# Three edits around waits in a two-layer decoder trunk: a norm matmul four blocks later, a normalization spread over more blocks, a rearranged end

## The chip, the cores and the metric

One core of one Trainium2 chip. The metric is the device time of one execution in microseconds, given as the median of several runs. The core has a matmul engine (PE, with its weight loads PEld), a vector engine (DVE), an activation engine (ACT), GpSimd (POOL) and a queue engine (SP) that issues transfers. Each engine works through its own instructions in order and waits on semaphores for the others.

## What is computed

Two layers over 256 tokens of width 2048, all in fp32. Layer 0 mixes with attention heads and gated linear attention, layer 1 with a Mamba-2 mixer; after each comes a squared-ReLU MLP and a per-layer input embedding, and at the end a norm:

```python
for i in range(DEPTH):
    hn = rms_norm(h, norm_mix[i])
    h = h + (sb_gla_mixer if i % 2 == 0 else ssd_mixer)(hn, ...)
    h = h + squared_relu_mlp(rms_norm(h, norm_mlp[i]), mlp_w_up[i], mlp_w_down[i])
    h = h + sigmoid(h @ ple_w_gate[i]) * (p[i] @ ple_w_proj[i])
return rms_norm(h, final_norm)
# in ssd_mixer, before the output projection:
#   z, xbc, dt = split(hn @ w_in); xbc = silu(causal_conv(xbc)); y = scan(xbc, softplus(dt))
#   y = rms_norm((y + d * xs) * silu(z), norm_g);  return y @ w_out
```

A norm is a row's values times `rstd`, one number per token (the reciprocal root of the mean square), times a gain per column. Since `rstd` is one number per token, a projection may be taken first of the values with the gain alone and be multiplied by `rstd` afterwards. The kernel uses that in places: `xu` holds the layer's input with the gain but without `rstd`, `x` holds it with both.

## The kernel before

Every fp32 product is made of three reduced-precision products: a weight block is split into a high part (`whi`, a cast on ACT, line 84) and the remainder (`wlo`, a subtraction on DVE, line 85), and the activations were split in the same way earlier (`split_into`, a scaled copy on ACT, line 105, and a multiply-subtract on DVE, line 106). So each 128x1024 piece of weights that PE uses needs one pass of ACT and then one of DVE. Three buffers each hold `whi` and `wlo`.

The weights stream through two loops. `feature_major` (PE lines 124 and 129) gives transposed results, four PSUM banks for each group of 512 columns, out of a pool of five banks; `token_major` (PE lines 153 to 155) gives rows, two banks for each group. Both are generators that yield after every block of 1 MB of weights and once more after a group's evacuation. `pace` drives such a generator and, after each of its yields, advances a list of side generators by one step: `[start, every, generator]`. That is how normalization, convolution, scan and statistics are laid between the weight blocks. The order of the text is a wish only: a scheduler that works at compile time orders the instructions of each engine by readiness in its own model, so that an instruction which depends on nothing can move far ahead.

Second mixer (`mixer1`). Its steps are counted in yields of `main`. Yields 1 to 5 are the first group (B), 6 to 10 the second (C), 11 and 12 the `dt` block, all three on `xu`, with the results multiplied by `rstd` afterwards (lines 166 and 167). Yields 13 to 17 are the first group of `xs`, on `x`, and all later groups use `x`. `norm_x` starts at yield 2: it makes `rstd` out of the sums of squares (`h_rstd`, `rstd_rows`), and then `normalize` makes `x`: for each of 16 slices one multiplication on POOL (`hn`, line 258) and one `split_into`. Two slices are made for each yield, in yields 4 to 11. Beside it run the convolution steps of B and C (`conv_silu`, lines 505 to 510), the `dt` chain (`dt_steps`, lines 466 to 494, on DVE) and, from yield 18, the scan of group 0 (`group`).

Pages of 8 KB per partition come from one pool of 12 (`pages`): four for `x`, four for `xu`, two for `raw`, one each for `bc`, `dt_work`, `rb`, `mt` and so on.

End of the second mixer. `sq_acc`, the sum of squares of the gated result, is built up by `gated` on POOL (line 181). `y_rstd` (line 673) sums it over channels by a matmul with one column (line 676) and makes `r_y`. It is carried over into the output projection as a side that starts at its first yield. `r_y` is read by the first evacuation there, after eight blocks (line 311).

The end. In the second layer's `ple`, each of four column groups ends in an evacuation for each of two token halves: sigmoid on ACT (line 379), multiplication and addition on DVE (lines 382 and 383), and a square with a row sum on ACT (line 229). ACT needs a table load before a function that the loaded set does not have. Line 381 applies a square root to a constant column, in the last evacuation of the text. After the loop, `h_rstd` makes the last `rstd`, and eight DVE instructions (line 397) multiply 128x512 pieces by it and by the final gain, each followed by a transfer of 256 KB (line 398).

Of the kernel before, what the change touches and what calls it, by code (L numbers as in the profile page):

```python
# [11 lines left out]
AF = mybir.ActivationFunctionType  # L12
ALU = mybir.AluOpType
# [3 lines left out]
P = 128  # L17
T = 256
D = 2048
# [6 lines left out]
def hybrid_trunk(  # L26
# [25 lines left out]
    nc = tc.nc  # L52
# [9 lines left out]
    def small_ps(cols=512, name="sm"):  # L62
        return sm_ps.tile([P, cols], F32, tag="sm", name=name, padded_shape=[P, 512])

    h = keep.tile([P, 2, D], F32, name="h")
# [7 lines left out]
    one_col = keep.tile([P, 1], F32, name="one_col")  # L73
    nc.gpsimd.memset(one_col, 1.0)
    warm = keep.tile([P, 1], F32, name="warm")
# [3 lines left out]
    rstd = keep.tile([P, T], F32, name="rstd")  # L79
# [19 lines left out]
    def split_into(x_tile, value, g=None):  # L99
        hi, lo = x_tile[:, 0:T], x_tile[:, T : 2 * T]  # L100
        if g is None:
            nc.scalar.copy(out=hi, in_=value)
            nc.vector.tensor_tensor(out=lo, in0=value, in1=hi.bitcast(F32), op=ALU.subtract)
        else:
            nc.scalar.activation(hi, value, AF.Copy, scale=g)
            nc.vector.scalar_tensor_tensor(out=lo, in0=value, scalar=g, in1=hi.bitcast(F32), op0=ALU.mult, op1=ALU.subtract)  # L106
# [120 lines left out]
    def square_rows(t, g):  # L227
        junk = ev.tile([P, 512], F32, tag="row", name="junk")
        nc.scalar.activation(junk, h[:, t, g * 512 : (g + 1) * 512], AF.Square, accum_out=ssq[:, t, g : g + 1])

    def page(shape, name, dt=F32):
        return pages.tile(shape, dt, tag="pg", name=name, padded_shape=[P, 2048] if len(shape) == 2 else None)
# [5 lines left out]
    def new_x():  # L238
        return operand(4, "x")

    def hand_on(g, xt, which=None, raw=None):

        for k in range(4 * g, 4 * g + 4, 2):
            tp = small_ps(512, "x_tp")
            for j in range(2):
                for t in range(2):
                    nc.tensor.transpose(tp[:, j * T + t * P : j * T + t * P + P], h[:, t, (k + j) * P : (k + j + 1) * P], ident)  # L247
            for j in range(2):
                split_into(xt(k + j), tp[:, j * T : (j + 1) * T], None if which is None else gain[:, which, k + j : k + j + 1])
            if raw is not None:  # L250
                nc.scalar.copy(out=raw[k // 8][:, k % 8 : k % 8 + 2, :].rearrange("p k t -> p (k t)"), in_=tp)
            yield

    def normalize(x, raw, which, step=2):

        for k in range(KT):
            hn = ev.tile([P, T], F32, tag="t", name="hn")
            nc.gpsimd.tensor_tensor(out=hn, in0=raw[k // 8][:, k % 8, :], in1=rstd, op=ALU.mult)
            split_into(x(k), hn, gain[:, which, k : k + 1])
            if (k + 1) % step == 0:  # L260
                yield

    def grid(ap, groups, kb_n):
        return [[ap[g * kb_n + kb] for kb in range(kb_n)] for g in groups]
# [93 lines left out]
    def ple(i, x, px):  # L358

        last = i == 1  # L360
        nxt = None if last else new_x()
        raw = None if last else [page([P, 8, T], f"hT{m}") for m in range(2)]
        pps = page([P, 2, 2, 512], "pp")
        sides = []
        if last:
            fg = page([P, D], "fg")
            nc.scalar.dma_start(fg, final_gain.partition_broadcast(P))

        def main():
            for g in range(4):  # L370
                pp = pps[:, g % 2]

                def evac_pp(_, t, bank):
                    nc.scalar.copy(out=pp[:, t, :], in_=bank)

                def evac(_, t, bank):
                    cs = slice(g * 512, (g + 1) * 512)
                    e = ev.tile([P, 512], F32, tag="row", name="e_pg")
                    nc.scalar.activation(e, bank, AF.Sigmoid)
                    if last and g == 3 and t == 1:  # L380
                        nc.scalar.activation(warm, one_col, AF.Sqrt)
                    nc.vector.tensor_tensor(out=e, in0=e, in1=pp[:, t, :], op=ALU.mult)
                    nc.vector.tensor_tensor(out=h[:, t, cs], in0=h[:, t, cs], in1=e, op=ALU.add)
                    square_rows(t, g)

                yield from token_major([[ple_proj[i, g]]], 1, lambda k: px[:, k, :], evac_pp, kts=2)
                yield from token_major(grid(ple_gate[i], [g], 4), 4, x, evac)
                if not last:
                    sides.append([None, 1, hand_on(g, nxt, 1, raw)])

        pace(main(), sides, last=last)
        if last:
            r = h_rstd("r_out")
            for g in range(3, -1, -1):
                for t in range(2):
                    hs, fs = h[:, t, g * 512 : (g + 1) * 512], fg[:, g * 512 : (g + 1) * 512]
                    nc.vector.scalar_tensor_tensor(out=hs, in0=hs, scalar=r[:, t : t + 1], in1=fs, op0=ALU.mult, op1=ALU.mult)
                    (nc.sync if t else nc.scalar).dma_start(out[:, t, g * 512 : (g + 1) * 512], hs)
        return nxt, raw

    def sb_head(hh, q, k, v, o_tile, tmp, neg_tri, neg_ones):
# [38 lines left out]
    def mixer1(xu, raw):  # L440
        with tc.tile_pool(name="mix1", bufs=1) as mid, tc.tile_pool(name="mix1t", bufs=2) as tmp:
# [11 lines left out]
            x = new_x()  # L453
# [43 lines left out]
            def conv_in(bank, scale=None):  # L497
                xp = tmp.tile([P, T + 4], F32, tag="xp", name="xp", bufs=5)
                nc.gpsimd.memset(xp[:, 0:3], 0.0)
                add_halves(xp[:, 3 : T + 3], bank, scale=scale)  # L500
                return xp
# [91 lines left out]
            def gated(g, sz):  # L593
                for j in range(4):
                    gate_silu(sz[:, j, :], sz[:, j, :])
                    y = y_of(4 * g + j)
                    nc.gpsimd.tensor_tensor(out=y, in0=y, in1=sz[:, j, :], op=ALU.mult)
                    square_acc(g == 0 and j == 0, y)
                    yield

            def fm(nb, evac, xt=x):
                return feature_major(grid(ssd_in, nb, 4), 4, xt, evac)

            def norm_x():
                r = h_rstd("r_mix")
                yield from rstd_rows(r)
                yield from normalize(x, raw, 1)

            sides = [[2, 1, norm_x()]]
            bc, xs, sz, todo = {}, {}, {}, []  # L610
# [11 lines left out]
            def evac_x(g):  # L622
                def evac(n, bank):
                    if n == 0:
                        xs[g] = tmp.tile([P, 4, T], F32, tag="xs", name="xs")
                    todo.append((xs[g][:, n, :], 4 * g + n, conv_in(bank)))
                    if n == 3:
                        sides.append([None, 1, conv_silu(todo[-4:])])
                return evac
# [21 lines left out]
            def main():  # L651
                for g in range(8):
                    half = g // 4
                    if g % 4 == 0:
                        yield from fm([16 + half], evac_bc(half, 0), x if half else xu)
                        yield from fm([18 + half], evac_bc(half, 1), x if half else xu)
                    if g == 0:
                        yield from feature_major([[ssd_dt]], 1, xu, evac_dt, width=1, kts=16)
                    yield from fm([8 + g], evac_x(g))
                    sides.append([None, 1, group(g, bc[half][:, g % 4, :], bc[half][:, 4 + g % 4, :], xs[g])])  # L660
                    if g:
                        yield from fm([g - 1], evac_z(g - 1))
                        sides.append([None, 1, gated(g - 1, sz[(g - 1) // 2][:, 4 * ((g - 1) % 2) :, :])])
                sides.append([None, 1, split_y(0, 12)])
                yield from fm([7], evac_z(7))
# [5 lines left out]
            scale = []  # L671

            def y_rstd():
                ms = small_ps(2, "ms")
                for c in range(2):
                    nc.tensor.matmul(ms[:, c : c + 1], lhsT=sq_acc[:, c * P : (c + 1) * P], rhs=one_col,
                                     start=(c == 0), stop=(c == 1), skip_group_check=True)
                scale.append(rstd_cols(ms, 4096, "r_y"))
                yield
# [253 lines left out]
    x = None  # L933
    for i in range(2):
        x = mixer1(x, raw) if i else mixer0()
        x, px = mlp(i, x)
        x, raw = ple(i, x, px)
# [66 lines left out]
```

## Time and profile before

| | us |
|---|---|
| median of three runs | 2767.04 |
| lowest and highest of them | 2765.21, 2768.29 |
| the profiled execution | 2768.19 |
| span of its instructions | 2766.5 |
| mean granted TensorE clock | 0.996 |

The profile gives, for one execution, each instruction's start and length, what an engine had waited for before it, and the clock that TensorE was granted (1.0 is the 2.4 GHz level, 0.5 the 1.2 GHz level). Ends of matmuls are modelled. 1.7 us of the execution lie outside the span.

### The profile page before, as it was taken

To read this page: it belongs to the slowest core of one execution; us is meant where nothing else is said; L and a number is where in the kernel's file an instruction comes from. 1 tells how busy PE (TensorE), PEld (TensorE's weight loads), DVE (VectorE), ACT (ScalarE), POOL (GpSimd) and SP (SyncE) were. 2 spreads that over 40 slices of the span, in tenths; PEclk is the share of its full clock that TensorE was granted. 3 is DMA by queue.
4 is the path that set the end of the run, shared out by engine and by line. 5 is a ranking of instruction groups with operands and counts; after the bars stand their busy time and mean duration, and the time that the engine had idled before them with its cause. 6 is when DMAs were issued, how large, how long until landed. Compare 5 with 4: busy or idle time off the path is not lost.

```text
span 2766.5 us, 35708 instructions
## 1 busy us (share of the span) xinstructions
PE 2723.0 (98%) x14120; PEld 2298.0 (83%) x14120; DVE 1721.3 (62%) x2394; ACT 1370.4 (50%) x1942; POOL 165.7 (6%) x258
## 2 busy tenths in 40 slices
PE   8999999999999999998999999999999999999997
PEld 6888878888888888887888888788888888888886
DVE  7455666665555655568887888754666565565555
ACT  6455455443444434566555565644444344443444
POOL 3000000000000000002132122300000000000000
PEclk9999999999999999999999999999999999999999
DMA  6544355555555555454554555455555555555554
GB/s 248 194 154 166 122 185 185 193 186 198 184 197 188 196 192 188 175 193 142 205 197 174 182 196 183 153 184 196 183 193 188 197 184 197 186 199 190 190 190 145
DMA packets 73880, 511.68 MB, mean 185 GB/s; under 512 B 8736, under 2 KB 8928, under 8 KB 13040
## 3 DMA queue, kind: packets, MB, share of 16 engines
q1 hardware_dynamic: 70928, 498.63, 51.1%
q10 hardware_dynamic: 2784, 10.78, 1.1%
q8 instruction: 110, 1.80, 0.3%
q14 instruction: 58, 0.48, 0.0%
HBM read 507.21 MB, written 2.16 MB: 184 GB/s over the span
## 4 chain that ended last, share of the span: by engine, by line
PE 94%; DVE 4%; ACT 1%; issue 1%; POOL 0%; DMA 0%; POOLq 0%; DVEq 0%; ACTq 0%
PE acc L124 31%; PE acc L129 15%; PE acct L155 15%; PE acct L153 15%; PE acct L154 15%; DVE wlo L85 1%; PE x_tp L247 1%; PE y_ps L578 1%; DVE yx L106 1%; PE y_ps L580 0%; DVE x L106 0%; ACT whi L84 0%; DVE a_cv L508 0%; PE gla_o L880 0%; PE xs_tp L554 0%
## 5 line engine op out<-in xcount | busy, mean ns | idle before, releaser
L85 DVE TENSOR_TENSOR wlo<-wraw,whi 128x1024 fp32r<-128x1024 f32 x940 | 1161.0, 1236 | 946.5 <-ACT whi L84 945.0
L84 ACT CAST whi<-wraw 128x1024 fp32r<-128x1024 f32 x940 | 987.9, 1052 | 1187.7 <-PE acct L155 638.0
L124 PE MATMUL acc<-x,whi 128*128 128x512 f32 x3872 | 1223.7, 399 | 11.7 <-ACT whi L84 9.5
L129 PEld LDWEIGHTS acc<-x,wlo 128*128 128x128 f32 x3872 | 723.9, 189 | 181.6 <-DVE wlo L85 13.9
L129 PE MATMUL acc<-x,wlo 128*128 128x256 f32 x3872 | 760.1, 279 | 9.6 <-DVE wlo L85 9.6
L124 PEld LDWEIGHTS acc<-x,whi 128*128 128x128 f32 x3872 | 596.7, 189 | 21.3 <-ACT whi L84 9.7
L155 PE MATMUL acct<-whi,hid 128*128 128x512 f32 x1024 | 399.6, 390 | 0.0
L153 PE MATMUL acct<-whi,hid 128*128 128x512 f32 x1024 | 399.1, 390 | 0.0
L154 PE MATMUL acct<-wlo,hid 128*128 128x512 f32 x1024 | 398.5, 389 | 0.0
L155 PEld LDWEIGHTS acct<-whi,hid 128*128 128x128 f32 x1024 | 192.6, 188 | 39.7
L154 PEld LDWEIGHTS acct<-wlo,hid 128*128 128x128 f32 x1024 | 192.2, 188 | 39.7
L153 PEld LDWEIGHTS acct<-whi,hid 128*128 128x128 f32 x1024 | 192.3, 188 | 39.2
L153 PE MATMUL acct<-whi,x 128*128 128x512 f32 x384 | 150.7, 392 | 0.0
L154 PE MATMUL acct<-wlo,x 128*128 128x512 f32 x384 | 149.7, 390 | 0.0
L155 PE MATMUL acct<-whi,x 128*128 128x512 f32 x384 | 149.7, 390 | 0.0
L155 PE MATMUL acct<-whi,yx 128*128 128x512 f32 x256 | 101.2, 395 | 0.0
L153 PE MATMUL acct<-whi,yx 128*128 128x512 f32 x256 | 100.8, 394 | 0.0
L154 PE MATMUL acct<-wlo,yx 128*128 128x512 f32 x256 | 100.6, 393 | 0.0
L164 ACT COPY right<-acc 128x256 f32<-128x256 f32 x198 | 72.2, 368 | 27.6 <-PE acc L129 27.1
L155 PEld LDWEIGHTS acct<-whi,x 128*128 128x128 f32 x384 | 72.1, 188 | 15.1
L153 PEld LDWEIGHTS acct<-whi,x 128*128 128x128 f32 x384 | 72.1, 188 | 14.5
L154 PEld LDWEIGHTS acct<-wlo,x 128*128 128x128 f32 x384 | 72.1, 188 | 14.4
(259 smaller groups left out, 1848.2 us busy)
## 6 DMA issues: line engine op xcount, KB each, us to landing
wraw<-in_mlp_up_dram SPq DMA_DIRECT2D x128, 1024.0 KB, 4.8
wraw<-in_mlp_down_dram SPq DMA_DIRECT2D x128, 1024.0 KB, 4.8
wraw<-in_ssd_in_dram SPq DMA_DIRECT2D x80, 1024.0 KB, 4.8
wraw<-in_ab_in_dram SPq DMA_DIRECT2D x47, 1024.0 KB, 4.9
wraw<-in_ple_gate_dram SPq DMA_DIRECT2D x32, 1024.0 KB, 4.8
wraw<-in_ssd_out_dram SPq DMA_DIRECT2D x32, 1024.0 KB, 4.8
wraw<-in_ab_out_dram SPq DMA_DIRECT2D x16, 1024.0 KB, 4.8
rb<-acs_rows ACTq DMA_DIRECT2D x8, 1024.0 KB, 5.0
```

Source lines behind the costliest of these rows:

```text
L84: nc.scalar.copy(out=hi, in_=src_raw)
L85: nc.vector.tensor_tensor(out=lo, in0=src_raw, in1=hi.bitcast(F32), op=ALU.subtract)
L106: nc.vector.scalar_tensor_tensor(out=lo, in0=value, scalar=g, in1=hi.bitcast(F32), op0=ALU.mult, op1=ALU.subtract)
L124: nc.tensor.matmul(banks[n], lhsT=hi[:, o : o + P], rhs=xt(k), start=(k == 0), stop=False, skip_group_check=True)
L129: nc.tensor.matmul(banks[n][:, T : 2 * T], lhsT=lo[:, o : o + P], rhs=xt(k)[:, 0:T], start=False, stop=(k == kb_n * kts - 1), skip_group_c ...
L153: nc.tensor.matmul(banks[n], lhsT=xh, rhs=wh, start=(k == 0), stop=False, skip_group_check=True)
L154: nc.tensor.matmul(banks[n], lhsT=xh, rhs=wl, start=False, stop=False, skip_group_check=True)
L155: nc.tensor.matmul(banks[n], lhsT=xl, rhs=wh, start=False, stop=(k == kb_n * kts - 1), skip_group_check=True)
L164: nc.scalar.copy(out=right[:rows], in_=bank[:rows, T : 2 * T])
L247: nc.tensor.transpose(tp[:, j * T + t * P : j * T + t * P + P], h[:, t, (k + j) * P : (k + j + 1) * P], ident)
L578: nc.tensor.matmul(y_ps[64 * u : 64 * u + 64, c * P : c * P + P], lhsT=xdt[:, c, 64 * r : 64 * r + 64], rhs=mt[:, r, c, :], start=(c == 0) ...
```

## The change

Three places change. In `mixer1`, `normalize` makes one slice for each yield instead of two, so it runs in yields 4 to 19; the first group of `xs` therefore takes `xu` in place of `x`, and its results are multiplied by `rstd` when they are evacuated. `y_rstd` waits for four yields before its first instruction. In the last layer's `ple`, the product with the final gain is taken when a column group is finished, into two new pages `hg`; both halves' squares and products come after the second half's addition; the square root on a constant is replaced by a table load that is tied to stand behind the last sigmoid on ACT; and the end multiplies four pieces of 128x1024 by `rstd`, the first on ACT and three on DVE, each followed by a transfer of 512 KB.

```diff
         if last:
             fg = page([P, D], "fg")
             nc.scalar.dma_start(fg, final_gain.partition_broadcast(P))
+            hg = [page([P, D], f"hg{t}") for t in range(2)]
...
                 def evac(_, t, bank):
                     cs = slice(g * 512, (g + 1) * 512)
                     e = ev.tile([P, 512], F32, tag="row", name="e_pg")
-                    nc.scalar.activation(e, bank, AF.Sigmoid)
+                    sig = nc.scalar.activation(e, bank, AF.Sigmoid)
                     if last and g == 3 and t == 1:
-                        nc.scalar.activation(warm, one_col, AF.Sqrt)
+                        with tc.issue_after(sig.ins):
+                            nc.scalar.preload_act_table_set("sqrt_and_others")
                     nc.vector.tensor_tensor(out=e, in0=e, in1=pp[:, t, :], op=ALU.mult)
                     nc.vector.tensor_tensor(out=h[:, t, cs], in0=h[:, t, cs], in1=e, op=ALU.add)
-                    square_rows(t, g)
+                    for u in (range(2) if t else ()) if last else (t,):
+                        square_rows(u, g)
+                        if last:
+                            nc.vector.tensor_tensor(out=hg[u][:, cs], in0=h[:, u, cs], in1=fg[:, cs], op=ALU.mult)
...
             r = h_rstd("r_out")
-            for g in range(3, -1, -1):
-                for t in range(2):
-                    hs, fs = h[:, t, g * 512 : (g + 1) * 512], fg[:, g * 512 : (g + 1) * 512]
-                    nc.vector.scalar_tensor_tensor(out=hs, in0=hs, scalar=r[:, t : t + 1], in1=fs, op0=ALU.mult, op1=ALU.mult)
-                    (nc.sync if t else nc.scalar).dma_start(out[:, t, g * 512 : (g + 1) * 512], hs)
+            for t, c in ((0, 0), (1, 0), (0, 1), (1, 1)):
+                part = hg[t][:, c * 1024 : (c + 1) * 1024]
+                if t == 0 and c == 0:
+                    nc.scalar.activation(part, part, AF.Copy, scale=r[:, t : t + 1])
+                else:
+                    nc.vector.tensor_scalar(out=part, in0=part, scalar1=r[:, t : t + 1], scalar2=None, op0=ALU.mult)
+                (nc.sync if t else nc.scalar).dma_start(out[:, t, c * 1024 : (c + 1) * 1024], part)
...
             def norm_x():
                 r = h_rstd("r_mix")
                 yield from rstd_rows(r)
-                yield from normalize(x, raw, 1)
+                yield from normalize(x, raw, 1, 1)
...
-                    todo.append((xs[g][:, n, :], 4 * g + n, conv_in(bank)))
+                    todo.append((xs[g][:, n, :], 4 * g + n, conv_in(bank, None if g else rstd)))
...
-                    yield from fm([8 + g], evac_x(g))
+                    yield from fm([8 + g], evac_x(g), x if g else xu)
...
             def y_rstd():
+                for _ in range(4):
+                    yield
                 ms = small_ps(2, "ms")
```

## Rows read from the trace of the kernel before

**Rows 1.** Windows of 70 us: busy PE, PEld, DVE, ACT, POOL; clock, DMA share, GB/s.
```profile
1260.00:1330.00 70.00, 60.13 (x318) 50.39 (x318) 63.13 (x113) 40.95 (x68) 12.52 (x24) 0.95 0.45 154
1750.00:1820.00 70.00, 65.39 (x300) 52.88 (x299) 44.90 (x65) 37.37 (x60) 11.48 (x11) 0.95 0.47 165
```

**Rows 2.** PE's timeline around `y_rstd`: start, length, line; idle before and its releaser.
```profile
1775.27 1.01 PE L676 MATMUL ms<-one_col,sq_acc 128*128 128x1 f32 x4 [4.57 <-POOL sq_acc L181]
```

**Rows 3.** Window behind that matmul, same columns as rows 1.
```profile
1775.30:1780.50 5.20, 5.20 (x15) 4.29 (x16) 1.54 (x3) 2.24 (x2) 0.00 (x0) 0.51 0.09 36
```

**Rows 4.** Timeline, ACT and DVE, up to the first reader of `r_y`.
```profile
1792.93 1.05 ACT L84 CAST whi<-wraw 128x1024 fp32r<-128x1024 f32 x1 [1.67 <-PE acct L155]
1808.76 1.40 DVE L311 SCALAR_TENSOR_TENSOR h<-acct,r_y,h 128x512 f32<-128x512 f32 x2
```

**Rows 5.** Windows of the second mixer's start, same columns as rows 1.
```profile
1262.00:1272.00 10.00, 7.78 (x36) 6.56 (x35) 8.11 (x15) 5.09 (x9) 0.82 (x2) 0.83 0.37 118
1272.00:1312.00 40.00, 32.36 (x174) 26.95 (x173) 39.42 (x71) 26.70 (x46) 10.18 (x20) 0.97 0.36 128
1312.00:1340.00 28.00, 28.00 (x158) 23.72 (x158) 22.50 (x45) 15.47 (x24) 1.45 (x5) 0.99 0.70 247
1340.00:1400.00 60.00, 60.00 (x374) 50.55 (x374) 54.79 (x111) 35.17 (x57) 16.47 (x21) 1.00 0.51 184
```

**Rows 6.** Timeline of the first stall there: POOL, ACT, PE.
```profile
1256.72 4.04 POOL L258 TENSOR_TENSOR hn<-hT,rstd 128x256 f32<-128x256 f32 x4 [904.66 <-ACT rstd L224]
1261.22 1.03 ACT L84 CAST whi<-wraw 128x1024 fp32r<-128x1024 f32 x1
1264.42 0.81 PE L124 MATMUL acc<-x,whi 128*128 128x512 f32 x2 [2.23 <-DVE xp L165]
```

**Rows 7.** Window, instructions on tile `x` alone: busy PE, PEld, DVE, ACT.
```profile
1262.00:1312.00 50.00, 40.13 (x208) 33.51 (x207) 5.76 (x13) 5.99 (x12) 0.94 0.37 126
```

**Rows 8.** DVE's timeline: a subtraction beside POOL, one alone, the `rstd` multiplication.
```profile
1280.27 1.76 DVE L85 TENSOR_TENSOR wlo<-wraw,whi 128x1024 fp32r<-128x1024 f32 x1
1268.91 1.23 DVE L85 TENSOR_TENSOR wlo<-wraw,whi 128x1024 fp32r<-128x1024 f32 x1 [0.28 <-ACT whi L84]
1264.62 0.74 DVE L167 TENSOR_TENSOR xp<-xp,rstd 128x256 f32<-128x256 f32 x2
```

**Rows 9.** Timeline of the kernel's start: ACT and PE.
```profile
11.64 1.28 ACT L381 ACT_TABLE_LOAD   x1
28.69 0.20 ACT L197 ACTIVATE root<-ms_eps 128x2 f32<-128x2 f32 x1 [0.43 <-DVE ms_eps L194]
30.12 0.71 PE L223 MATMUL r_row<-diag,ones 128*128 128x128 f32 x4 [0.88 <-DVE diag L217]
```

**Rows 10.** Timeline of the end: PE, ACT, DVE, ACT's transfers.
```profile
2750.93 0.39 PE L155 MATMUL acct<-whi,x 128*128 128x512 f32 x1
2752.70 0.58 ACT L379 ACTIVATE e_pg<-acct 128x512 f32<-128x512 f32 x1
2754.04 0.69 DVE L383 TENSOR_TENSOR h<-h,e_pg 128x512 f32<-128x512 f32 x1
2755.51 1.28 ACT L197 ACT_TABLE_LOAD   x1
2756.80 0.20 ACT L197 ACTIVATE root<-ms_eps 128x2 f32<-128x2 f32 x1
2757.82 5.39 DVE L397 SCALAR_TENSOR_TENSOR h<-h,r_out,fg 128x512 f32<-128x512 f32 x8
2758.61 4.31 ACTq L398 DMA_DIRECT2D out_dram<-h  x4
```

**Rows 11.** Window of the last transfers, same columns as rows 1.
```profile
2759.50:2765.00 5.50, 0.00 (x0) 0.00 (x0) 3.71 (x6) 0.00 (x0) 0.00 (x0) 0.50 1.01 378
```

**Rows 12.** Groups by line and form: busy, mean ns: DVE's scalar multiplications.
```profile
L217 DVE TENSOR_SCALAR diag<-ident,r_mix 128x128 f32<-128x128 f32 x4 | 1.0, 284 | 0.1
L485 DVE TENSOR_SCALAR dt_work<-dt_work,neg_a 64x256 f32<-64x256 f32 x1 | 0.3, 345 | 0.0
```

## The prediction

> **What bounds the kernel now.** I read windows of 70 us first. PE is busy without a gap nearly everywhere, so what an edit can win lies in the stretches where PE stands still or runs at the lower clock. The two rows of [rows 1] are such stretches: 9.87 us and 4.61 us without PE, both at a mean clock of 0.95. A third is the end, where PE has finished and everything is a chain, and a fourth is the start. Then I read each place with finer windows and the timeline of each engine, to see which wait ends last there. The change touches all four places, the start without naming it.
>
> **The late matmul.** PE stands for 4.57 us before the matmul of `y_rstd`, waiting for POOL's last addition into `sq_acc` [rows 2]. Behind it come 5.20 us at a granted clock of 0.51, the 1.2 GHz level [rows 3], which is half of full speed: 2.55 us more are lost. Together 7.1 us. The weights' products that stand behind the matmul need nothing from it. Moved by four blocks, it stands where? ACT's casts show the pace of the output projection: 1.05 us plus 1.67 us idle, 2.72 us for half a block [rows 4], so four blocks are 21.8 us, and the matmul comes near 1792. `sq_acc` is complete at 1775.2, some 17 us earlier. `r_y` is first read at 1808.76 [rows 4], some 16 us later. What moves along with it is a table load of 1.28 us (as in [rows 10]), one root on ACT and five tiny DVE steps; they fit one of ACT's gaps of 1.67 us, and three buffers of `whi` cover what spills over. If that cover were gone, PE would lose about 1.3 us. What is late next is DVE: beside POOL a subtraction takes 1.76 us in place of 1.23 [rows 8], and with a slice of the last `yx` in between DVE needs slightly more than 2.72 us for half a block, for two or three half blocks. I take back 0.6 us for that. Gain 6.5 us, bounds 5.0 and 7.1.
>
> **The normalization.** PE loses 2.22 us in 1262 to 1272 and 7.64 us in 1272 to 1312, and the clock (0.83 and 0.97) costs 1.7 and 1.2 us more: 12.8 us [rows 5]. There are two causes. The first stall: ACT's next cast starts only at 1261.22, behind four scaled copies that wait for four products of POOL (4.04 us from 1256.72); the evacuation of the first group's banks stands behind that cast, and PE waits 2.23 us for a bank [rows 6]. With one slice for each yield two of the four products fall away before that cast, so the cast and the evacuation come about 2.0 us earlier, nearly the whole stall. Then DVE: it is busy for 39.42 of 40 us from 1272 to 1312 while PE is not [rows 5], so there each microsecond of DVE work is one of the kernel.
>
> What does DVE save up to there? From 1262 on, thirteen instructions on `x` cost 5.76 us, 0.44 each [rows 7]; at half the pace four fewer lie in the stretch, 1.8 us. Four fewer products on POOL also slow DVE less: the difference between 1.76 and 1.23 [rows 8] was hit by about four of some twelve products, with smaller hits beside, so I put it at 0.22 each, 0.9 us. With the first stall gone, the 1.89 us that DVE is idle in 1262 to 1272 [rows 5] go too. With the 2.0 us of the earlier cast this makes 6.6 us.
>
> The work isn't gone, it comes later. Seven slices at 0.44 plus 0.22 us and four multiplications of the new evacuation (0.74 for two, [rows 8]) are 6.1 us, and they land in 1305 to 1345. There DVE has 5.5 us free until 1340 and 5.2 us from 1340 to 1400, while PE has no gap [rows 5]. It fits, narrowly; I take back 0.6 us. Gain 6.0 us. The lower bound is 1.5 us, if only the four instructions and nothing of the stall count; the upper one is 9, if the lower clock also stays away. That `x` of slice 15 is made at yield 19 and read by the block ahead of yield 21 leaves one to two blocks of about 5.5 us (two halves at the pace of [rows 4]).
>
> **The end.** The last half of the projection ends near 2751.32, but the second sigmoid starts at 2752.70, behind the first square [rows 10]. In the new order it starts at 2751.34 and ends at 2751.94. DVE has the first half's addition until 2752.05, then needs two passes of 0.69 with 0.03 between: the second half is added at 2753.48 instead of 2754.73. The table load runs at 2751.95 to 2753.23 under these, the two squares until 2754.79 at the latest (before, a square with its row sum had the 0.78 us between the addition's end, 2754.73, and the load), and DVE's two products with the gain, 0.69 each, end at 2754.90. So the row sums go into `rstd` at 2754.92; two tiny steps, at 0.2 us each as the five between the root and the first final product (1.02 us in all), bring the root to 2755.30. Before, the load held it until 2756.80 [rows 10]. The first final product starts at 2756.32 instead of 2757.82. That is 1.5 us earlier, although DVE's products now lie on the path. For the final pieces, one scalar multiplication takes 0.284 us for 128 columns and 0.345 us for 256 [rows 12]; continued, 1024 columns are an estimate of 0.71 us, about the 0.74 us from the first product's step before. The transfers then set the end: 378 GB/s without a gap for 5.5 us [rows 11]. They carry the same 2.1 MB, start 1.5 us earlier and are fed faster than they drain. Longer runs may help a little. Gain 1.6 us, bounds 0.8 (were the pieces to take one column per step, 1.2 us, the first transfer loses 0.5) and 2.2. The eight products of earlier groups lie behind PE's work and cost nothing: DVE is free for half of that stage; without that cover they would be 5.5 us.
>
> **The start, which pays.** Line 381's root depends on nothing and was moved by the scheduler to 11.64 us, the start of the kernel [rows 9]. So it did nothing for the end; but it left the root table loaded for the first norm, whose root at 28.69 has no load ahead of it [rows 9]. The change takes it away. Then the load of 1.28 us stands before that root. ACT is idle for 0.43 us there, so 0.85 to 0.9 us are added to a chain that PE is already waiting for (0.88 us before `r_row`, [rows 9]). The 1.5 us that ACT saves at 11.64 help nobody, since PE has no gap there. Cost 0.9 us, bounds 0 and 2.8: the upper one if the longer stall drops the clock as the 2.23 us of [rows 6] did, where 10 us at 0.83 [rows 5] cost 1.7.
>
> What does a load hold up? Here the root follows the load's end within 0.01 us [rows 10], so 1.28 us is all that I count, in both places. The Trainium skill, "ScalarE: Activation LUTs", section "What ACT_TABLE_LOAD costs", puts a switch at about 2.66 us, 1.28 for the load and 1.38 for a drain. By that page the start would pay 2.3 us, and at the end, where both squares now stand behind the load, the gain would shrink by 1.3 us; the sum would be 10.5 us. The row speaks against it.
>
> **The sum.** 6.5 + 6.0 + 1.6 - 0.9 = 13.2 us. Against the profiled execution, 2768.19 us (span 2766.5 and 1.7 outside it), this gives 2755.0. That execution lies 1.15 us above the median of 2767.04, so for a median I say 2754.0, with 2749.5 to 2758 as this case's own range.
>
> **Rivals.**
> - Chance 0.62: the forecast.
> - The normalization returns little (0.18): DVE stays the bound until 1345, the deferred 6.1 us meet a DVE that has no lead, and PE stands there instead. For it speaks that DVE's room until 1340 is smaller than what is added. Gain 1.5 us there: about 2758.5, or 2760 with the clock at the start.
> - All stalls go (0.08): 9 us there and the upper bounds elsewhere: 2748.
> - The matmul's move does nothing (0.05), because the scheduler puts it as far forward as its model says `sq_acc` is ready, as it did with line 381. Against it: it now stood behind what the text has ahead of it, not ahead. Without 6.5 us: 2760.5.
> - A load holds ACT for twice its 1.28 us (0.02), as a drain behind it would: the start pays 2.2 us, the end wins 0.3, in all 10.6 us: 2756.5. Only the row of [rows 10], with nothing behind the load, speaks to it. This is what the Trainium skill's page above would come to.
> - Slower (0.05): `xu` must stay until the first group of `xs` is read, and `dt_work` is taken before that. Counted, four pages of `x`, four of `xu`, two of `raw`, one of `bc` and this one are exactly the 12. If one page more is still held then, `dt_work` waits for `xu` to be read, four blocks or 22 us, with DVE's subtractions queued behind it. Three buffers of `wlo` cover three halves, 8.2 us; PE stands for 14, loses 2 more to the clock, and the 6 us of the normalization are gone: 8.8 us slower, about 2776. The count decides, and it just fits.
>
> **How the numbers follow.** The likeliest case gives 2754.0. From 2749 to 2760.5 only the best case (0.08), the slower one (0.05) and a part of the matmul's case are left out. About 0.2%, 5.5 us, is what a measurement of this kernel can tell from no change: faster by that, below 2761.5, 0.90; within it 0.05; slower 0.05.
>
> **What would show it.** Right: the column matmul near 1785 with no wait and no clock of 0.5 around it; PE busy for more than 66 of the 70 us from 1260; a table load ahead of the root near 28.3 and PE idle for 1.7 us or more there; the last load ended before the last addition; a first transfer 5.8 us behind the last matmul's end, where it was 7.3 [rows 10]. Wrong: PE waits on `wlo` between 1312 and 1400, which had none, or on `x` at the second group; a transfer rate below 378 GB/s at the end.

## The result, and the profile after

The changed kernel takes 2753.00 us in the median (2751.97 to 2753.93) against 2767.04 (2765.21 to 2770.09): ratio 0.9948, 95% interval 0.9932 to 0.9964. Faster by 14.0 us, with 2754.0 forecast. The execution that was profiled with these times, and one of `after_late1` below, ran throughout at a clock of 0.56; with them the two medians would be 2753.86 and 2761.26 instead of 2753.00 and 2760.72. The rows below are of a second set of executions of the changed kernel, `after_again` below: span 2752.2, 2753.9 with what lies around it.

Windows of the changed kernel (columns as in [rows 1]), over the start, the places of [rows 1] and [rows 5], and a window around the late matmul:

```profile
28.00:36.00 8.00, 5.77 (x26) 4.62 (x25) 5.16 (x9) 5.86 (x8) 3.33 (x3) 0.79 0.28 93
1260.00:1330.00 70.00, 64.69 (x359) 55.62 (x358) 68.05 (x123) 44.27 (x76) 18.14 (x29) 0.95 0.49 169
1262.00:1272.00 10.00, 10.00 (x59) 8.69 (x58) 9.90 (x20) 7.37 (x13) 1.12 (x3) 1.00 0.42 119
1272.00:1312.00 40.00, 34.69 (x189) 30.02 (x188) 39.84 (x70) 24.97 (x43) 13.04 (x20) 0.91 0.46 158
1312.00:1340.00 28.00, 28.00 (x160) 23.85 (x159) 26.76 (x60) 17.51 (x28) 3.82 (x8) 1.00 0.64 236
1340.00:1400.00 60.00, 60.00 (x378) 50.37 (x376) 54.38 (x105) 37.12 (x61) 18.59 (x21) 1.00 0.52 184
1760.00:1800.00 40.00, 39.96 (x178) 32.02 (x177) 26.40 (x30) 22.16 (x33) 6.87 (x7) 1.00 0.57 201
```

The window from 1760 is full at full clock. The first stall, 1262 to 1272, is full too. But from 1272 to 1312 PE is busy for 34.69 of 40, only 2.33 more than before, at 0.91, and DVE for 39.84: the stretch is still DVE's. The start has lost 0.89 us of PE and some clock, as the same two windows of the kernel before show:

```profile
28.00:36.00 8.00, 6.66 (x38) 5.54 (x37) 6.18 (x12) 6.46 (x11) 3.45 (x3) 1.00 0.25 93
1760.00:1800.00 40.00, 35.39 (x146) 28.31 (x145) 23.44 (x31) 18.11 (x26) 10.84 (x10) 0.91 0.47 164
```

Timeline of PE in the changed kernel: the first norm, the one wait at the second mixer's start, and the late matmul (start, length, line; idle before and its releaser):

```profile
30.24 0.71 PE L223 MATMUL r_row<-diag,ones 128*128 128x128 f32 x4 [1.76 <-DVE diag L217]
31.42 2.93 PE L124 MATMUL acc<-x,whi 128*128 128x512 f32 x6 [0.47 <-ACT whi L84]
1303.62 2.08 PE L129 MATMUL acc<-x,wlo 128*128 128x256 f32 x8 [5.31 <-DVE wlo L85]
1779.99 0.50 PE L685 MATMUL ms<-one_col,sq_acc 128*128 128x1 f32 x4
```

The matmul of [rows 2] now has no wait ahead of it. The stall of [rows 6] is gone. In place of it and of four waits on `wlo` in the kernel before (1.42, 2.14, 1.41 and 2.67 us, 9.87 us of PE's idle time with the 2.23) there is a single one of 5.31 us. In the kernel before, the matmuls behind `r_row` and the four waits:

```profile
31.30 1.66 PE L124 MATMUL acc<-x,whi 128*128 128x512 f32 x6 [0.47 <-ACT whi L84]
1286.96 0.50 PE L129 MATMUL acc<-x,wlo 128*128 128x256 f32 x2 [1.42 <-DVE wlo L85]
1296.33 1.22 PE L129 MATMUL acc<-x,wlo 128*128 128x256 f32 x8 [2.14 <-DVE wlo L85]
1303.76 1.22 PE L129 MATMUL acc<-x,wlo 128*128 128x256 f32 x8 [1.41 <-DVE wlo L85]
1309.49 2.08 PE L129 MATMUL acc<-x,wlo 128*128 128x256 f32 x8 [2.67 <-DVE wlo L85]
```

What the late `wlo` was behind, in the changed kernel's timeline of ACT and DVE:

```profile
1294.81 1.04 ACT L84 CAST whi<-wraw 128x1024 fp32r<-128x1024 f32 x1
1291.30 1.21 DVE L85 TENSOR_TENSOR wlo<-wraw,whi 128x1024 fp32r<-128x1024 f32 x1
1299.32 1.74 DVE L481 RECIPROCAL dt_work<-dt_work 64x256 f32<-64x256 f32 x1
1302.35 1.21 DVE L85 TENSOR_TENSOR wlo<-wraw,whi 128x1024 fp32r<-128x1024 f32 x1
```

Its `whi` stood at 1295.85. DVE, never idle, came to the subtraction at 1302.35: conv steps, a slice of `x` and the first part of `dt_steps`, with the reciprocal, stand ahead of it in DVE's order.

ACT at the start of the changed kernel, then the end (PE, ACT, DVE, SP's transfers, and the window of the transfers):

```profile
27.51 1.28 ACT L197 ACT_TABLE_LOAD   x1
28.81 0.20 ACT L197 ACTIVATE root<-ms_eps 128x2 f32<-128x2 f32 x1
...
2738.68 0.39 PE L155 MATMUL acct<-whi,x 128*128 128x512 f32 x1
2739.11 0.60 ACT L380 ACTIVATE e_pg<-acct 128x512 f32<-128x512 f32 x1 [0.76 <-PE acct L155]
2739.72 1.28 ACT L383 ACT_TABLE_LOAD   x1
2740.95 0.68 DVE L385 TENSOR_TENSOR h<-h,e_pg 128x512 f32<-128x512 f32 x1
2742.82 0.20 ACT L197 ACTIVATE root<-ms_eps 128x2 f32<-128x2 f32 x1 [0.43 <-DVE ms_eps L194]
2743.84 2.08 DVE L404 TENSOR_SCALAR hg<-hg,r_out 128x1024 f32<-128x1024 f32 x3
2744.62 1.67 SPq L405 DMA_DIRECT2D out_dram<-hg  x2
2745.40:2750.65 5.25, 0.00 (x0) 0.00 (x0) 0.52 (x1) 0.00 (x0) 0.00 (x0) 0.50 1.01 399
```

From the last matmul's start to the end of the span 13.52 us pass (2752.2 - 2738.68), where it was 15.57 (2766.5 - 2750.93, [rows 10]): 2.05 us less.

### The profile page after: what moved, and what is told of

Same layout as the page of the kernel before. It is cut to its first block, busy times and chain, and to the rows that moved or that the text cites. A ratio compares the mean times of both kernels' runs of the same rounds, so it can differ in the third digit from the quotient of the medians.

```text
span 4525.2 us, 35706 instructions
## 1 busy us (share of the span) xinstructions
PE 4502.7 (100%) x14120; PEld 2916.1 (64%) x14120; DVE 1742.9 (39%) x2401; ACT 1380.2 (30%) x1942; POOL 158.3 (3%) x258
## 4 chain that ended last, share of the span: by engine, by line
PE 100%; ACT 0%; DMA 0%; DVE 0%; DVEq 0%; issue 0%; ACTq 0%
PE acc L124 33%; PE acc L129 17%; PE acct L154 15%; PE acct L155 15%; PE acct L153 15%; PE x_tp L247 1%; PE y_ps L585 1%; PE y_ps L587 0%; PE xs_tp L561 0%; PE st_ps L576 0%; PE gla_o L889 0%; PE z L423 0%; PE sc L876 0%; PE gla_o L885 0%; PE gms L896 0%; PE z L410 0%
## 5 line engine op out<-in xcount | busy, mean ns | idle before, releaser
L124 PE MATMUL acc<-x,whi 128*128 128x512 f32 x3872 | 1862.2, 578 | 9.4 <-ACT whi L84 9.4
L129 PEld LDWEIGHTS acc<-x,wlo 128*128 128x128 f32 x3872 | 844.6, 219 | 597.3 <-issue 296.8
L129 PE MATMUL acc<-x,wlo 128*128 128x256 f32 x3872 | 1111.4, 384 | 0.0
L124 PEld LDWEIGHTS acc<-x,whi 128*128 128x128 f32 x3872 | 814.7, 229 | 55.2 <-issue 16.8
L155 PE MATMUL acct<-whi,hid 128*128 128x512 f32 x1024 | 592.3, 578 | 0.0
L153 PE MATMUL acct<-whi,hid 128*128 128x512 f32 x1024 | 590.1, 576 | 0.0
L154 PE MATMUL acct<-wlo,hid 128*128 128x512 f32 x1024 | 589.9, 576 | 0.0
L155 PEld LDWEIGHTS acct<-whi,hid 128*128 128x128 f32 x1024 | 223.9, 219 | 168.7 <-issue 99.2
L153 PEld LDWEIGHTS acct<-whi,hid 128*128 128x128 f32 x1024 | 224.0, 219 | 165.3 <-issue 96.4
L153 PE MATMUL acct<-whi,x 128*128 128x512 f32 x384 | 216.4, 563 | 0.0
L154 PE MATMUL acct<-wlo,x 128*128 128x512 f32 x384 | 215.1, 560 | 0.0
L155 PE MATMUL acct<-whi,x 128*128 128x512 f32 x384 | 214.9, 560 | 0.0
L155 PE MATMUL acct<-whi,yx 128*128 128x512 f32 x256 | 148.2, 579 | 0.0
L153 PE MATMUL acct<-whi,yx 128*128 128x512 f32 x256 | 147.9, 578 | 0.0
```

The costliest lines, as they stand in the source:

```text
L124: nc.tensor.matmul(banks[n], lhsT=hi[:, o : o + P], rhs=xt(k), start=(k == 0), stop=False, skip_group_check=True)
L129: nc.tensor.matmul(banks[n][:, T : 2 * T], lhsT=lo[:, o : o + P], rhs=xt(k)[:, 0:T], start=False, stop=(k == kb_n * kts - 1), skip_group_c ...
L153: nc.tensor.matmul(banks[n], lhsT=xh, rhs=wh, start=(k == 0), stop=False, skip_group_check=True)
L154: nc.tensor.matmul(banks[n], lhsT=xh, rhs=wl, start=False, stop=False, skip_group_check=True)
L155: nc.tensor.matmul(banks[n], lhsT=xl, rhs=wh, start=False, stop=(k == kb_n * kts - 1), skip_group_check=True)
```

## The experiments

The theory is the prediction's: four places that add up. Its rivals: the normalization returns little, or the matmul's move does nothing. The first four kernels take the change apart.

**The changed kernel again** (no edit).

> The changed kernel once more, without any edit, to have a profile of it at full clock. Theory (three gains and one cost: the late matmul 6.5 us, the normalization 6.0, the end 1.6, the start minus 0.9): about 2754 us; PE idle for more than 1.7 us near 28 to 32 us, no wait ahead of the column matmul, PE busy for more than 66 of the 70 us from 1260. Rival (the normalization gives little, something else gave the gain): the 70 us from 1260 still show about 60 us of PE.

Measured: 2753.49 us (2752.28 to 2755.25), ratio 0.9953 (0.9938 to 0.9968); the kernel before had 2766.38 beside it.

**The late matmul alone**, in the kernel before:

```diff
             def y_rstd():
+                for _ in range(4):
+                    yield
                 ms = small_ps(2, "ms")
```

> The kernel before with one edit: the norm's column matmul starts four yields later. Theory: 6.5 us less than before (5.0 to 7.1), 2760.5 us; the wait of 4.6 us and the 5 us at half clock behind it are gone. Rival (the scheduler leaves the matmul where it was): no difference, 2767 us, the wait still there. Rival (DVE's subtractions are the bound there once the wait is gone): 3 us or less.

Measured: 2759.24 (2758.72 to 2762.47), ratio 0.9978 (0.9969 to 0.9988): 7.1 us less. Its windows:

```profile
1260.00:1330.00 70.00, 60.11 (x329) 50.55 (x328) 64.40 (x115) 42.04 (x71) 11.95 (x25) 0.98 0.48 166
1760.00:1800.00 40.00, 39.96 (x175) 31.87 (x174) 25.53 (x29) 19.98 (x28) 9.37 (x9) 1.00 0.55 197
```

The second is what the whole change shows there, so the place's gain is all this edit's, and it is the full stall and its clock. DVE takes nothing back.

**The normalization alone**, in the kernel before:

```diff
-                yield from normalize(x, raw, 1)
+                yield from normalize(x, raw, 1, 1)
...
-                    todo.append((xs[g][:, n, :], 4 * g + n, conv_in(bank)))
+                    todo.append((xs[g][:, n, :], 4 * g + n, conv_in(bank, None if g else rstd)))
...
-                    yield from fm([8 + g], evac_x(g))
+                    yield from fm([8 + g], evac_x(g), x if g else xu)
```

> The kernel before with one edit: one slice of the second mixer's normalization for each yield, and the first group of xs on the input without rstd. Theory: 6.0 us less than before (1.5 to 9), 2761 us; no stall of 2.2 us near 1262, PE idle for about 4 us in place of 9.9 from 1260 to 1330. Rival (DVE stays the bound and the deferred work meets a DVE without lead): 1.5 us less, 2765.5 us, with PE waiting on wlo between 1312 and 1345.

Measured: 2761.32 (2759.35 to 2762.36), ratio 0.9979 (0.9970 to 0.9989): 5.1 us less. PE's only wait from 1255 to 1340, and the window:

```profile
1300.63 2.08 PE L129 MATMUL acc<-x,wlo 128*128 128x256 f32 x8 [4.79 <-DVE wlo L85]
1260.00:1330.00 70.00, 65.21 (x357) 56.05 (x357) 67.47 (x127) 43.82 (x73) 19.95 (x28) 0.95 0.50 171
```

The new wait comes with this edit, so it is no product of the whole.

**The end alone** (the diff's parts of `ple`, with the constant's root taken out), in the kernel before.

> The kernel before with one edit: the rearranged end, which also takes away the square root on a constant column that had run at the kernel's start. Theory: 1.6 us gained at the end, 0.9 lost at the start, 0.7 us less than before in all, 2766.3 us; from the last matmul's end to the first transfer 5.8 us in place of 7.3. Rival (the longer stall at the start drops the clock): 1 us more than before, 2768 us.

Measured: 2768.87 (2763.83 to 2772.10), ratio 1.0006 (0.9997 to 1.0015): 2.5 us more in the median, though the interval includes no difference. Against the 0.7 us less of the theory it is a miss. The profiled execution (span 2762.1), the fastest of the ten, has the shorter end, 13.48 us from the last matmul's start. Its windows:

```profile
28.00:36.00 8.00, 5.78 (x33) 4.80 (x32) 5.62 (x11) 6.95 (x9) 3.20 (x2) 1.00 0.29 90
1260.00:1330.00 70.00, 59.98 (x337) 50.39 (x336) 64.31 (x117) 42.83 (x72) 14.20 (x27) 1.00 0.48 167
```

The start pays 0.88 us here too, but at full clock, and the second stretch has PE as idle as before at 1.00 instead of 0.95. Executions with the same waits there differ by such drops. So the next two ask what the start costs.

**The constant's root back**, in the changed kernel and in the end alone:

```diff
                         with tc.issue_after(sig.ins):
                             nc.scalar.preload_act_table_set("sqrt_and_others")
+                        nc.scalar.activation(warm, one_col, AF.Sqrt)
```

> The changed kernel with one line back: the Sqrt on a constant behind the sigmoids of the preload, which in the kernel before let the root's table be loaded at 11.64 us, under the first transfers. Theory (the load directly ahead of the first root costs 0.88 us of TensorE's time between 28 and 36 us, 6.66 us busy before and 5.77 after, and in some runs the clock falls there too): the first norm has no table load ahead of its root, TensorE's idle time on r_row is back at 0.9 us from 1.8, 6.66 of the 8 us from 28 to 36 are busy at clock 1.00, and the time is 0.9 to 2.6 us below that of the changed kernel, so 2751 to 2752.7 beside 2753.6; the end keeps its gain, because there the table is loaded anyway behind the second sigmoid. Rival (the start's stall is made up later by buffers that fill ahead): no difference, 2753.6. Second rival: the line's removal was needed for the end, whose table load then comes later again: 2754.2.

> The kernel before with the rearranged end alone, the Sqrt on a constant kept. The rearranged end without that Sqrt gave +2.5 us in the median against the kernel before, although its end is about 2.05 us shorter in the traces (13.1 us from the last matmul to the span's end against 15.2) and its start only 0.88 longer. Theory (the rest of the loss, 3.6 us, is a lower granted clock that follows the longer stall at the start in most of its runs): with the Sqrt back the end's 2.05 us are all that remains, 2764.3 beside 2766.4. Rival (the loss has nothing to do with the start, but with the clock in the other stalls, which fall out differently from run to run): 2767 to 2769, no better than without the Sqrt.

Measured: 2751.57 (2750.76 to 2751.83), ratio 0.9943 (0.9930 to 0.9955), beside 2753.49 without it; and 2765.54 (2763.76 to 2767.63), ratio 0.9993 (0.9984 to 1.0002), beside 2768.87. So the root's removal costs 1.9 us in the one and 3.3 in the other, more than the 0.88 of the longer wait: for the start the theory holds, and the rivals of no difference fall. The end's 2.05 us don't show in full in the medians: `end_warm` lies 1.1 us below the kernel before beside it (2766.63), where 2764.3 was expected, and its interval includes no difference. `after_warm` at the start:

```profile
28.64 0.20 ACT L197 ACTIVATE root<-ms_eps 128x2 f32<-128x2 f32 x1 [0.43 <-DVE ms_eps L194]
28.00:36.00 8.00, 6.66 (x38) 5.55 (x37) 6.22 (x12) 6.46 (x11) 3.49 (x3) 1.00 0.29 98
```

No load ahead of the root, and 6.66 us at full clock, as before the change.

**The pace of two slices again**, with `xu` kept for the first group:

```diff
-                yield from normalize(x, raw, 1, 1)
+                yield from normalize(x, raw, 1)
```

> The changed kernel with the normalization of the second mixer at two tiles per step again, as before the change, but with the first group of blocks still reading the un-normalized tiles. It tells whether the pace or the un-normalized operand carries the 5.1 us that the part alone returned. Theory (the pace: POOL's products of 4.04 us and ScalarE's share of the normalization come within half the blocks and are what delayed the cast and the addition at 1261 us): the wait of 2.2 us on xp is back and the clock falls with it, 3 to 5 us slower than the changed kernel, 2756.5 to 2758.5. Rival (the operand: once the first group doesn't read the normalized tiles, when they are written matters to nobody): within 1 us of the changed kernel, 2753 to 2754.5.

Measured: 2761.27 (2756.30 to 2761.94), 7.8 us above the changed kernel: the pace carries the gain, and more than expected. PE's waits from 1255 to 1320, first and last of five:

```profile
1266.37 0.72 PE L124 MATMUL acc<-x,whi 128*128 128x512 f32 x2 [2.22 <-DVE xp L165]
...
1312.70 1.21 PE L129 MATMUL acc<-x,wlo 128*128 128x256 f32 x8 [2.66 <-DVE wlo L85]
```

They sum up to 9.82 us, as before the change. The pace of two slices without `xu` is the old code; the pace of one slice without `xu` wasn't tried, since the first group would read `x` before all of it is written.

**`dt_steps` two yields later**, in the changed kernel:

```diff
             def dt_steps(work):
+                for _ in range(2):
+                    yield
                 u, e, s, q, dt, acs, chunk_keep = (work[:, i, :] for i in range(7))
```

> The changed kernel with the chain of steps for dt (its first part ends in a reciprocal of 1.74 us on VectorE) begun two blocks later. In the changed kernel TensorE waits once for 5.3 us, near 1298, on a wlo that VectorE writes at 1302.35 though its wraw and whi stood at 1295.85; in VectorE's order the dt steps, the conv of the blocks before and slices of the normalized tiles stand ahead of it. Theory (the dt steps in front of that wlo are what makes it late: 0.83, 0.28, 1.74, 0.41 and 0.41 = 3.7 us of the 6.5): the wait shrinks to under 2 us, and with it the low clock from 1300 to 1308; 3 to 5 us faster, 2748.5 to 2750.5. Rival (VectorE is full in that stretch, 11.96 of 12 us, so that what leaves one wlo stands ahead of the next): the wait breaks into smaller ones of the same sum, within 1 us of the changed kernel, and gains only where the clock no longer falls. Second rival: the rows of acs come later and the first group's broadcast is late, a wait on rb, 2 us slower.

Measured: 2752.65 (2750.62 to 2753.41), ratio 0.9946 (0.9933 to 0.9958): 0.8 us less than the changed kernel, the rival's size and not clear of the spread, for the executions of the two overlap. All PE waits from 1255 to 1345, and the window:

```profile
1299.82 0.50 PE L129 MATMUL acc<-x,wlo 128*128 128x256 f32 x2 [1.32 <-DVE wlo L85]
1303.74 0.50 PE L129 MATMUL acc<-x,wlo 128*128 128x256 f32 x2 [0.86 <-DVE wlo L85]
1316.52 0.73 PE L124 MATMUL acc<-x,whi 128*128 128x512 f32 x2 [1.11 <-DVE xp L165]
1325.53 1.21 PE L129 MATMUL acc<-x,wlo 128*128 128x256 f32 x8 [0.45 <-DVE wlo L85]
1339.01 1.21 PE L129 MATMUL acc<-x,wlo 128*128 128x256 f32 x8 [0.72 <-DVE wlo L85]
1260.00:1330.00 70.00, 66.25 (x374) 55.85 (x373) 68.55 (x124) 44.97 (x76) 21.69 (x29) 1.00 0.49 173
```

The dt steps did make the 5.31 us wait, for it breaks up with them: 3.29 us are left up to 1320, 4.46 with the two behind it, and no low clock. The work only moved, so the stretch stays DVE's.

**Both together**, the root back and `dt_steps` two yields later.

> The changed kernel with both edits that gained something beside it: the Sqrt on a constant kept at the start (1.9 us below the changed kernel in the medians, 2751.57 to 2753.49) and the dt steps begun two blocks later (0.8 us, 2752.65; its profile shows full clock from 1256 to 1400, and the wait of 5.3 us on wlo is replaced by ones of 1.32, 1.11 and 0.86). Theory (the two are in different stretches, and the runs of the second kernel above 2752.6 are those in which the clock falls at the start, which the first edit stops): the gains add, 2749.5 to 2750.5, with little spread. Rival (with another start the waits on wlo fall elsewhere, and the clock falls there): 2751 to 2752, no better than the first edit alone.

Measured: 2750.07 (2749.96 to 2750.70), ratio 0.9941 (0.9929 to 0.9954). All its executions lie below all of the changed kernel's; the two gains add (0.8 and 1.9 below 2753.49 make 2750.8), and the spread is under 1 us. Its windows, both at full clock:

```profile
28.00:36.00 8.00, 6.65 (x38) 5.55 (x37) 6.72 (x10) 6.58 (x10) 4.32 (x3) 1.00 0.44 156
1260.00:1330.00 70.00, 66.21 (x374) 55.84 (x373) 68.61 (x127) 44.94 (x75) 21.39 (x28) 1.00 0.52 179
```

**The column matmul one yield later, and two**, in the changed kernel (`range(4)` in `y_rstd` replaced by one or two).

> The changed kernel with the column matmul one block later instead of four. In the changed kernel POOL's last sum of squares begins at 1768.6 and takes 0.73 us, so it stands at 1769.4; a block is 16 matmuls of 0.227 us, 3.63 us, and the matmul stands at 1779.8 after four of them, so at 1765.2 without a delay, 1768.9 after one and 1772.5 after two. Theory (the matmul waits for that sum and for nothing else): TensorE waits 0.5 to 1.2 us, no low clock or a short one, 0.5 to 2 us slower than the changed kernel, 2754 to 2755.5. Rival (the sum itself moves, as it is behind work on POOL that waits for buffers of the blocks): the full wait of 4.6 us is back, 2758 to 2760. Second rival (one block is enough): 2753.5, no wait at all.

> The changed kernel with the column matmul two steps later instead of four. One step moved it by nothing: in TensorE's order it stood where it had stood before the change, 56 matmuls into the projection, because the scheduler had put it there itself, 2 1/3 blocks of 24 matmuls in, and one step asks for less than that. Four steps put it 64 matmuls further, two put it 16 further, 16 x 0.227 = 3.63 us. Theory (the wait is what is left until POOL's last sum is done): the wait of 4.57 us shrinks by 3.63 to 0.94, without the 5 us of half clock behind it; 1 to 2 us slower than the changed kernel, 2754 to 2755.5. Rival (any wait there brings the low clock): 2756 to 2758. Second rival (the four steps helped by something else, such as where the root and its table load fall on ScalarE): the 4.57 us are back, 2760 to 2761.

Measured: 2760.72 for one (2759.58 to 2762.52), and 2756.15 (2754.54 to 2758.13) for two. PE at the matmul, one yield, then (another kernel) two:

```profile
1770.73 1.01 PE L684 MATMUL ms<-one_col,sq_acc 128*128 128x1 f32 x4 [4.57 <-POOL sq_acc L181]
```

```profile
1770.57 0.60 PE L685 MATMUL ms<-one_col,sq_acc 128*128 128x1 f32 x4 [0.75 <-POOL sq_acc L181]
```

My expectation for one yield was wrong: I took a block for 16 matmuls (it is 24) and the matmul's old place for the one that the text gives it. In PE's order it stands behind 56 matmuls of the projection before the change, behind 56 with one yield, 72 with two and 120 with four. Two and four yields are three and five blocks of 24, counted from the projection's start as the text has it; one yield asks for two blocks, 48, less than the 56 where the scheduler had put the matmul by itself. So with one the wait is back in full, 7.2 us in the median. With two it stands 16 matmuls further, 16 x 0.227 = 3.6 us, and 4.57 shrinks to 0.75, near the 0.94 expected. Its median lies 2.7 us above the changed kernel's, more than the 0.75 us explain. Of the 1.5 us between the spans of the two profiled executions 0.75 are this wait, and 0.95 come before 64 us, where the text of the two kernels is the same; what else lies in the medians is open.

## Why the prediction was right, step by step

**The late matmul** (6.5 forecast): 7.1 us alone, the upper bound. The step "I take back 0.6 us" for DVE was wrong: nothing is late next. So was the place: not four blocks of 2 x 2.72 us further, 21.8 us, but 64 matmuls, 14.5 us, because the delay counts from the text's place, and the scheduler had already put the matmul 32 behind that. It stands at 1780, not near 1785. The last addition on POOL begins at 1768.6, and 10 us of margin were left, so the error cost nothing. The rival of the scheduler undoing the move had 0.05. With four yields it lost. With one its outcome comes true: the matmul already stood later than the text asked, and the move does nothing.

**The normalization** (6.0): 5.1 us alone, within its bounds. The first stall went as worked out: 2.22 us, with the clock from 0.83 to 1.00. The 2.7 us of DVE's work held as well: PE waited 7.64 us from 1272 to 1312 before, 5.31 after, and 4.79 in `norm_only`. The mis-sized step is the sum of 6.6 us under "What does DVE save": it has the first stall twice, as the 1.89 us that DVE is idle in it and as the 2.0 us of the earlier cast. Without the 1.89 it makes 4.7, and PE won 4.56 us of the 70 from 1260, 5.08 in `norm_only`. What I did not expect is that the waits left over gather in one. DVE is busy for 39.84 of 40 us from 1272 to 1312, after 39.42: what it was given back was filled at once by the next instructions in its order, and a `wlo` that had stood behind some waited 6.5 us for its turn. I had looked for that wait behind 1312, where the deferred slices land. There it did fit: DVE rises from 22.50 to 26.76 of 28 and PE has no gap. So the rival "returns little", built on that place, falls, and PE's 66 us of 70 were missed at 64.69.

**The end** (1.6): 2.05 us, within its bounds. Relative to the last matmul's start, the second sigmoid was due at 0.41 and came at 0.43, the load at 1.02 and 1.04, the first final product at 5.39 and 5.16: 0.23 us earlier, since one product with the gain slipped in ahead of the second addition. The rest is the transfers: 399 GB/s where I had counted 378 [rows 11], about 0.25 us of 5.25. The estimate of 0.71 us for 1024 columns was 0.69 (2.08 for three).

**The start** (0.9 lost): 0.88 us on PE, `r_row`'s wait 1.76 after 0.88 [rows 9], the load directly ahead of the root. I kept the lower clock only as the upper bound, 2.8; it comes in some executions (2.93 us for six matmuls above, 1.66 in the kernel before), and the measured cost is 1.9 us. The profiles agree. I count the subtractions of `wlo` on DVE, which come in the same order in every kernel: the 18th starts at 59.67 to 60.94 us in the six kernels with the constant's root, at 60.96 and 61.01 in the two without it whose clock stayed up (`end_only`, `after_dt2`), and at 62.20 to 63.25 in the four without it whose clock fell; the means with and without, 60.29 and 62.23, lie 1.9 us apart. The root starts at 28.81, 0.02 us behind the load's end at 28.79. The Trainium skill, "ScalarE: Activation LUTs", section "What ACT_TABLE_LOAD costs", counts about 1.38 us more for a drain at a switch; by that the root would come at 30.17. The trace disagrees, and the rival with 0.02 falls.

**The sum.** 7.1 + 5.1 + 2.05 - 1.9 = 12.35, measured 12.9 to 14.0; the forecast of 13.2 had a term 0.9 too large and two too small by 0.6 and 0.45, with the start's loss 1.0 too small. So it came out right partly by errors that cancel.

Between the two profiled executions the four places account for nearly everything. DVE's subtractions mark the stretches again; the 426th and the 470th, around the second mixer's start, in the kernel before and then (another kernel) in the changed one:

```profile
1241.60 1.23 DVE L85 TENSOR_TENSOR wlo<-wraw,whi 128x1024 fp32r<-128x1024 f32 x1
1392.61 1.21 DVE L85 TENSOR_TENSOR wlo<-wraw,whi 128x1024 fp32r<-128x1024 f32 x1
```

```profile
1242.93 1.22 DVE L85 TENSOR_TENSOR wlo<-wraw,whi 128x1024 fp32r<-128x1024 f32 x1
1387.09 1.21 DVE L85 TENSOR_TENSOR wlo<-wraw,whi 128x1024 fp32r<-128x1024 f32 x1
```

So 6.85 us are won there, 6.71 from the 579th to the 618th, around the late matmul, and 2.05 at the end, while 1.43 are lost up to the 18th: 14.2 of the 14.3 us between the spans.

The same stretch bears on why the pace is worth 7.8 us in the medians of the changed kernel and 5.1 alone. In the profiles it is worth nearly the same: the stretch takes 151.0 us in the kernel before and 144.6 in `norm_only`, 150.8 in `after_step2` and 144.2 in the changed kernel, so 6.4 and 6.7 us. But with the old pace and nearly the same waits it also takes 149.5 in `late_only` and 148.2 in `end_only`, whose clock fell less or not at all. The medians mix executions of both kinds, and by how much was not taken apart.

The rival "slower", by the count of pages, left no trace: `dt_work` is written without a wait.

## What to carry to other kernels

Where one engine is busy without a gap, ask what comes next in its order when work is moved away: here DVE stayed full, 5.31 of PE's 7.64 us of waits were left, and they gathered at one operand that stood far back. Count a stall once: the wait of one engine and the idle time of another in the same stretch can be the same microseconds. Before an instruction is removed as useless, look where the scheduler had put it and what state it left behind (here a table, worth 1.9 us). And a delay written in the source counts from the text's place, and does nothing until it passes the place that the scheduler chose, so read that place from the trace first.

## What was not expected of the hardware

The same stall lowers the granted clock in one execution and not in another: the 1.76 us before `r_row` are followed by a window at 0.79 in `after_again` and at 1.00 in `end_only`, and nearly the same waits from 1260 (9.87 to 10.02 us) went at 0.95 in the kernel before, 0.98 in `late_only` and 1.00 in `end_only`. That goes far to explain why executions of one kernel lie up to 8 us apart, for the mean granted clock of each execution is on record, and 0.001 of 2766 us is 2.8 us. In `end_only` the fastest, 2763.83, has 0.997 and the five from 2769.16 to 2772.10 have 0.994. In the kernel before, those at 0.996 lie between 2765.02 and 2768.44 and those at 0.995 between 2769.58 and 2770.16, and `best`, at 0.998 to 0.999, has a spread under 1 us. It is not all: `after_dt2` spreads over 2.8 us at 0.998.

The final transfers ran at 399 GB/s with pieces of 1024 columns, at 378 with 512. Whether the size of the pieces or their smaller number does it was not tried.
